# Three blocks on one core: weights as the stationary operand in FFN steps 2 to 9 and in the second heads' queries and keys

## The chip, the core and the metric

The kernel runs on one core of one Trainium2 chip. The metric is the device time of one execution in microseconds (us): three runs gave 985.66, 987.0 and 992.59 us, median 987.0 us. The profiled execution took 987.64 us, of which the span of its instructions is 985.9 us.

## The reference

For 256 tokens of width 1024 in float32, the reference runs three residual blocks one behind the other: a first block with a mixer of convolution and forgetting attention, and the two layers of block 2, one with blockwise attention (moba) and one with differential attention (diff). Each ends in a gated feed-forward network (FFN). What the change touches is this:

```python
def swiglu_2(h, w_in, w_out):
    g, u = jnp.split(h @ w_in, 2, axis=-1)
    return (jax.nn.silu(g) * u) @ w_out
...
    q, k, v = jnp.split(h @ w_qkv, 3, axis=-1)
```

The hidden width of every FFN is 2816. Block 2 modulates its norms by shift, scale and gate vectors, `c_act @ ada_w[i] + ada_b[i]`, which depend on the inputs alone and not on the tokens' way through the blocks.

## The kernel before, in words

**Products in three parts.** A float32 operand is split into a high part (rounded to the type fp32r by ScalarE) and a low part (what is left, subtracted by VectorE). A product is high by high, high by low and low by high, three matmuls into one bank of PSUM. The tokens' transposed activations are `hT` (high `hTh`, low `hTl`); each 128x512 piece of weights, a unit, gets its tiles `hi`/`lo` (or `wp`, a second pool that is open in the FFNs) as it arrives.

**The usual way round.** In `product` and `triple` the 128 tokens of one half are the stationary operand and 512 columns of weights move past them. The result has tokens on the partitions. Where the next product contracts over those columns, TensorE has to transpose the result, 128x128 at a time, by a matmul against `ident` (recorded under L151; all other matmuls stand under L145).

**The FFN.** It has 11 steps of 256 hidden columns. In `up(s, h)` the 8 units of step s (256 gate and 256 up columns side by side) are used for token half h: 24 matmuls of 512 columns into one bank. `activate` then takes Silu on ScalarE, multiplies on VectorE, has two transposes made, and splits the result into a tile `pair`. `downs(s)` multiplies by 4 units of the second matrix: 24 matmuls of 512 columns, which add into four banks held through the whole FFN. Steps 0 and 1 go first; from step 2 on the order is `up(s, 0)`, `up(s, 1)`, then `downs(s-1)` up to s = 8; `up(9)` stands without one; step 10 and the last three `downs` end the FFN, one token half after the other.

**Queries and keys in block 2.** Heads 0 to 3 are made the usual way. Those of heads 4 to 7 already go the other way round in `turned_product`: 128 columns of weights are stationary and the 256 tokens move, so the result has the columns on the partitions and needs no transposes. Two banks hold four heads' results, and `keep_turned` copies them out on ScalarE, 512 columns at a time.

**The order.** Every engine's order is fixed when the program is built. The class `Order` keeps a clock of its own, which the matmuls drive; after each matmul `pump` lets the waiting tasks (activations, softmax, `ada`) issue their next instruction, and then `fill` issues the splitting of the next weights. `Lane` holds one engine's order and its costs. On the chip each engine goes through its list in order and waits where its inputs aren't there. SyncE's queue loads all weights, 16 pairs of `hi`/`lo` tiles and in the FFNs 8 more pairs hold those that are split ahead of use. The `ada` task spreads the modulation vectors' 192 multiply-adds on VectorE (`asum<-araw`) over the program; each of their 24 halves ends in four transposes or two matmuls on TensorE. PSUM has 8 banks; in an FFN four of them are the held ones.

Of the kernel before, what the change touches and what calls it, by code (L numbers as in the profile page):

```python
# [13 lines left out]
F32R = mybir.dt.float32r  # L14
AF = mybir.ActivationFunctionType
OP = mybir.AluOpType
# [4 lines left out]
P = 128  # L21
# [197 lines left out]
def block_kernel(ctx: ExitStack, tc: tile.TileContext, a: dict, onehot: bass.AP, out: bass.AP):  # L219
# [12 lines left out]
    def small(name, shape, dtype=F32):  # L232
        return cst.tile(shape, dtype, name=name)
# [20 lines left out]
    hT = (small("hTh", [P, NKT, 256], F32R), small("hTl", [P, NKT, 256], F32R))  # L254
# [152 lines left out]
    def turned_product(us, blocks, marks):  # L407

        for k, u in enumerate(us):
            for h in range(2):
                o.wait(marks[h][k // 4])
            u.uses = 1
            wh, wl = use(u)
            xh, xl = hT[0][:, k], hT[1][:, k]
            last = k == len(us) - 1
            for ps, cs in blocks:
                for i, c in enumerate(cs):  # L420
                    out, w = ps[:, i * 256:(i + 1) * 256], slice(c, c + P)
                    o.mm(out, wh[:, w], xh, k == 0 and i == 0, False, True)
                    o.pump()
                    o.mm(out, wh[:, w], xl, False, False, True)
                    o.pump()
                    t = o.mm(out, wl[:, w], xh, False, last and i == len(cs) - 1, True)
                    o.pump()
            u.pool.give(u.slot, t)
        return t
# [662 lines left out]
    def ffn(hm, gb, **kw):  # L1092
        ys = []
        acts, act_mark, us_of, dn = {}, {}, {}, {}
# [3 lines left out]
        def activate(s, h, ps):  # L1098
# [16 lines left out]
            act_mark[s, h].t = split(acts[s][:, h], acts[s][:, 2 + h], tp[:, :256])  # L1115
            banks.give(tp, act_mark[s, h].t)

# [8 lines left out]
        def down(s, h, n):  # L1126
            if s not in dn:
                dn[s] = take(1)
            o.wait(act_mark[s, h])
            for j in range(2):  # L1130
                c = slice(j * P, (j + 1) * P)
                t = triple(ys[h][n][0], acts[s][:, h, c], acts[s][:, 2 + h, c], dn[s][2 * j + n],
                           s == 0 and j == 0, s == STEPS - 1 and j == 1)
            if s == STEPS - 1:
                ys[h][n][1].t = t
            if h and n:
                pairs.give(acts[s], t)
# [11 lines left out]
        for s in range(2, STEPS - 1):  # L1149
            up(s, 0)  # L1150
            up(s, 1)
            if s - 1 < STEPS - LAG:
                downs(s - 1)
# [47 lines left out]
    def attention(l, hm, gb, **kw):  # L1201
# [14 lines left out]
        qk_mark = {(n, i, h): Mark() for n in range(2) for i in range(2) for h in range(2)}  # L1216
# [21 lines left out]
        def keep_turned(n, i, bs):  # L1238
            while qks.when() is None or qks.when() > o.now:
                yield o.now + 0.1  # L1240
            qk[n, i] = qks.take()
            for j, b in enumerate(bs):
                r = A.activation(qk[n, i][:, 2 * j:2 * j + 2], b.rearrange("p (j t) -> p j t", t=256), AF.Copy,
                                 scale=1.0 if i else d ** -0.5)
                banks.give(b, r)
            for h in range(2):
                qk_mark[n, i, h].t = r
# [3 lines left out]
        def head(n, j):  # L1251
            hd = n * 4 + j
            yield from o.until(tb_mark[hd // 2], *(qk_mark[n, i, h] for i in range(2) for h in range(2)))
# [36 lines left out]
        for i in range(2):  # L1290
            bs = [o.hold(banks) for _ in range(2)]
            t = turned_product(take(2), [(b, (2 * j * P, (2 * j + 1) * P)) for j, b in enumerate(bs)], hm)
            o.spawn(keep_turned(1, i, bs), t)
# [105 lines left out]
```

## Time and profile before

| | |
|---|---|
| median of three runs | 987.0 us |
| profiled execution | 987.64 us |
| span of its instructions | 985.9 us |
| TensorE busy | 976.0 us, 99% |
| weight loads busy | 805.9 us, 82% |
| VectorE busy | 739.6 us, 75% |
| ScalarE busy | 605.1 us, 61% |
| DMA engines busy, weights' queue | 67.9% |

The ends of matmuls are modelled in this profile, so a recorded matmul is longer than its share of the engine: a matmul's price is the distance from its start to the next one's start. TensorE's granted clock was 0.999 of its full speed over the span.

### The profile page before, as it was taken

The numbers are of one execution on the slowest core, as the hardware profiler recorded it, in microseconds if no ns is written. First come the engines' busy times: TensorE is split into PE (matmuls) and PEld (weight loads), VectorE is DVE, ScalarE is ACT, GpSimd is POOL, SyncE is SP. The second block draws the span as 40 slices with busy tenths as digits, with TensorE's granted clock in tenths as the row PEclk, the third lists the DMA queues.
The fourth block names the chain that finished last, engine by engine and source line by source line (L and its number), as shares of the span: only waits on it lengthen the run. The fifth ranks groups of instructions, "written<-read, shape, count | busy, mean of one in ns | idle before, by whom it ended". The sixth has DMA issues, their size and how long they took to land.

```text
span 985.9 us, 14069 instructions
## 1 busy us (share of the span) xinstructions
PE 976.0 (99%) x4826; PEld 805.9 (82%) x4826; DVE 739.6 (75%) x1470; ACT 605.1 (61%) x1286; POOL 35.4 (4%) x65
## 2 busy tenths in 40 slices
PE   9999999999999999999999999999999999999997
PEld 6888778888888878898888888888897888888885
DVE  6789789989888868887899888637766796464632
ACT  7756675765546437866775554537878785454631
POOL 1000000000000001000000000001000100000000
PEclk9999999999999999999999999999999999999999
DMA  7977777679988874784779989636542657556401
GB/s 244 345 240 263 258 281 238 232 226 344 349 279 303 300 272 170 270 297 153 243 223 324 349 287 322 224 106 222 180 137 82 198 196 261 200 166 206 161 22 44
DMA packets 143637, 227.22 MB, mean 230 GB/s; under 512 B 6087, under 2 KB 79028, under 8 KB 143564
## 3 DMA queue, kind: packets, MB, share of 16 engines
q1 hardware_dynamic: 143548, 226.30, 67.9%
q8 instruction: 38, 0.62, 0.3%
q14 instruction: 35, 0.29, 0.1%
q10 hardware_dynamic: 16, 0.00, 0.0%
HBM read 225.22 MB, written 2.63 MB: 231 GB/s over the span
## 4 chain that ended last, share of the span: by engine, by line
PE 90%; DMA 3%; DVE 3%; issue 2%; ACT 1%; SPq 0%; POOL 0%; DVEq 0%; POOLq 0%; ACTq 0%
PE bank L145 85%; PE bank L151 5%; DMA araw<-in_ada_w_dram 2%; DVE asum L89 1%; DVE lo L89 1%; DMA x<-in_x_dram 1%; DVE wp L89 0%; ACT hi L89 0%; SPq L137 0%; DMA raw<-in_w_in_dram 0%; DVE x L89 0%; DVE ch L89 0%; ACT junk L89 0%; POOL tiny L89 0%; ACT L89 0%
## 5 line engine op out<-in xcount | busy, mean ns | idle before, releaser
L89 DVE TENSOR_TENSOR lo<-raw,hi 128x512 fp32r<-128x512 f32 (+1 forms) x499 | 322.9, 677 | 35.8 <-ACT hi L89 34.1
L89 ACT ACTIVATE hi<-raw 128x512 fp32r<-128x512 f32 (+1 forms) x499 | 298.0, 621 | 59.8 <-PE bank L145 35.2
L145 PE MATMUL bank<-hi,hTh 128*128 128x512 f32 (+1 forms) x670 | 262.7, 392 | 0.5 <-ACT hTh L89 0.5
L145 PE MATMUL bank<-hi,hTl 128*128 128x512 f32 (+1 forms) x670 | 261.8, 391 | 0.2 <-DVE hTl L89 0.2
L145 PE MATMUL bank<-lo,hTh 128*128 128x512 f32 (+1 forms) x670 | 261.0, 389 | 0.0
L145 PE MATMUL bank<-hi,pair 128*128 128x512 f32 x528 | 173.5, 394 | 0.0
L89 DVE SCALAR_TENSOR_TENSOR asum<-araw,c_act,asum 128x512 f32<-128x512 f32 x192 | 143.3, 746 | 7.9 <-DMA araw<-in_ada_w_dram 7.2
L145 PEld LDWEIGHTS bank<-hi,hTl 128*128 128x128 f32 x670 | 125.9, 188 | 26.1 <-issue 1.3
L145 PEld LDWEIGHTS bank<-lo,hTh 128*128 128x128 f32 x670 | 126.0, 188 | 24.2 <-DVE lo L89 0.8
L145 PEld LDWEIGHTS bank<-hi,hTh 128*128 128x128 f32 x670 | 125.9, 188 | 24.2 <-ACT hTh L89 1.3
L145 PE MATMUL bank<-wp,hTh 128*128 128x512 f32 x388 | 120.4, 391 | 0.0
L145 PEld LDWEIGHTS bank<-hi,pair 128*128 128x128 f32 x528 | 98.0, 188 | 19.7 <-issue 0.2
L89 ACT ACTIVATE ep<-bank 128x256 f32<-128x256 f32 x66 | 25.4, 384 | 131.8 <-PE bank L145 131.3
L145 PE MATMUL bank<-lo,pair 128*128 128x512 f32 x264 | 103.6, 393 | 0.0
L89 ACT ACTIVATE wp<-raw 128x512 fp32r<-128x512 f32 x145 | 88.9, 630 | 22.4 <-PE bank L145 16.4
L89 DVE TENSOR_TENSOR wp<-raw,wp 128x512 fp32r<-128x512 f32 x145 | 95.2, 686 | 8.8 <-ACT wp L89 8.6
L145 PEld LDWEIGHTS bank<-wp,hTh 128*128 128x128 f32 x388 | 72.5, 188 | 15.1
L89 DVE TENSOR_TENSOR ep<-ep,bank 128x256 f32<-128x256 f32 x70 | 29.2, 417 | 66.7 <-ACT ep L89 66.4
L145 PE MATMUL bank<-wp,hTl 128*128 128x512 f32 x194 | 75.9, 391 | 0.0
L145 PE MATMUL bank<-wp,pair 128*128 128x512 f32 x288 | 75.8, 396 | 0.0
L145 PEld LDWEIGHTS bank<-wp,pair 128*128 128x128 f32 x288 | 53.0, 188 | 10.4
L89 DVE TENSOR_TENSOR pair<-bank,pair 128x256 fp32r<-128x256 f32 (+1 forms) x74 | 32.5, 439 | 37.3 <-ACT pair L89 36.7
(131 smaller groups left out, 953.6 us busy)
## 6 DMA issues: line engine op xcount, KB each, us to landing
araw<-in_ada_w_dram SPq DMA_DIRECT2D x96, 512.0 KB
raw<-in_ffn_w_in_dram SPq DMA_DIRECT2D x88, 512.0 KB
raw<-in_w_gate_up_dram SPq DMA_DIRECT2D x44, 512.0 KB
raw<-in_ffn_w_out_dram SPq DMA_DIRECT2D x22, 1024.0 KB
raw<-in_w_in_dram SPq DMA_DIRECT2D x16, 1024.0 KB
raw<-in_moba_w_qkv_dram SPq DMA_DIRECT2D x12, 1024.0 KB
raw<-in_diff_w_qkv_dram SPq DMA_DIRECT2D x12, 1024.0 KB
raw<-in_w_down_dram SPq DMA_DIRECT2D x11, 1024.0 KB
```

The lines of the kernel that those rows point to most:

```text
L89: self.order.pin(self, fn(out, *args, **kw))
L145: self.pin(self.pe, self.nc.tensor.matmul(out, lhsT, rhs, start=start, stop=stop, skip_group_check=shared))
L151: self.pin(self.pe, self.nc.tensor.transpose(out, src, ident))
```

## The change

`hTh` and `hTl` become the two halves of one tile `hTb`, so that the high and the low part of the 256 tokens of one row of pieces lie side by side. `turned_product` then makes one matmul of 512 columns (the weights' high part against both parts of the tokens; the left half of the bank gets high by high, the right half high by low) and one of 256 columns (the weights' low part against the tokens' high part, into the left half). The two halves of the bank are added on the way out. One bank now holds 128 columns of the result.

This serves heads 4 to 7 (two passes over the weights, two heads each), and, new, FFN steps 2 to 9: `up_turned` makes, for each 128 of the step's 256 hidden columns, a bank of gate and a bank of up columns. `activate_turned` copies both left halves out on ScalarE, adds both right halves on VectorE, takes Silu, multiplies and splits. The result has the hidden columns on its partitions already, as `downs` wants it.

```diff
--- before.py
+++ after.py
@@ -251,7 +251,8 @@
 
     pairs = ring(cst, "pair", 4, [P, 4, 256], F32R)
     x = [small(f"x{h}", [P, D]) for h in range(2)]
-    hT = (small("hTh", [P, NKT, 256], F32R), small("hTl", [P, NKT, 256], F32R))
+    hT_both = small("hTb", [P, NKT, 2, 256], F32R)
+    hT = hT_both[:, :, 0], hT_both[:, :, 1]
 
 
     stream = []
@@ -412,20 +413,15 @@
         for k, u in enumerate(us):
             for h in range(2):
                 o.wait(marks[h][k // 4])
-            u.uses = 1
             wh, wl = use(u)
-            xh, xl = hT[0][:, k], hT[1][:, k]
-            last = k == len(us) - 1
-            for ps, cs in blocks:
-                for i, c in enumerate(cs):
-                    out, w = ps[:, i * 256:(i + 1) * 256], slice(c, c + P)
-                    o.mm(out, wh[:, w], xh, k == 0 and i == 0, False, True)
-                    o.pump()
-                    o.mm(out, wh[:, w], xl, False, False, True)
-                    o.pump()
-                    t = o.mm(out, wl[:, w], xh, False, last and i == len(cs) - 1, True)
-                    o.pump()
-            u.pool.give(u.slot, t)
+            for ps, c in blocks:
+                w, last = slice(c, c + P), k == len(us) - 1
+                o.mm(ps, wh[:, w], hT_both[:, k].rearrange("p i t -> p (i t)"), k == 0, False, True)
+                o.pump()
+                t = o.mm(ps[:, :256], wl[:, w], hT[0][:, k], False, last, True)
+                o.pump()
+            if not u.uses:
+                u.pool.give(u.slot, t)
         return t
 
     allk = range(NKT)
@@ -1091,7 +1087,7 @@
 
     def ffn(hm, gb, **kw):
         ys = []
-        acts, act_mark, us_of, dn = {}, {}, {}, {}
+        acts, act_mark, turned_mark, us_of, dn = {}, {}, {}, {}, {}
         last = kw.pop("last", False)
         out_marks = None if last else marks2()
 
@@ -1112,8 +1108,40 @@
                     acts[s] = pairs.take()
                 else:
                     yield o.now + 0.1
-            act_mark[s, h].t = split(acts[s][:, h], acts[s][:, 2 + h], tp[:, :256])
+            c = slice(h * P, (h + 1) * P)
+            act_mark[s, h].t = split(acts[s][:, 0:2, c], acts[s][:, 2:4, c], tp[:, :256].rearrange("p (j t) -> p j t", t=P))
             banks.give(tp, act_mark[s, h].t)
+
+        def activate_turned(s, j, bg, bu):
+
+            e = yield from o.get(st)
+            g, u = e[:, :256], e[:, 256:512]
+            r = A.activation(g, bg[:, :256], AF.Copy)
+            r2 = A.activation(u, bu[:, :256], AF.Copy)
+            yield r
+            r = V.tensor_add(g, g, bg[:, 256:])
+            banks.give(bg, r)
+            yield max(r, r2)
+            r2 = V.tensor_add(u, u, bu[:, 256:])
+            banks.give(bu, r2)
+            yield max(r2, A.activation(g, g, AF.Silu))
+            r = V.tensor_mul(g, g, u)
+            yield r
+            while s not in acts:
+                if pairs.when() is not None and pairs.when() <= o.now:
+                    acts[s] = pairs.take()
+                else:
+                    yield o.now + 0.1
+            turned_mark[s, j].t = split(acts[s][:, j], acts[s][:, 2 + j], g)
+            st.give(e, turned_mark[s, j].t)
+
+        def up_turned(s):
+            us = take(2)
+            for j in range(2):
+                turned_mark[s, j] = Mark()
+                bs = [(o.hold(banks), c) for c in (j * P, 256 + j * P)]
+                t = turned_product(us, bs, hm)
+                o.spawn(activate_turned(s, j, bs[0][0], bs[1][0]), t)
 
         def up(s, h):
             if s not in us_of:
@@ -1126,10 +1154,10 @@
         def down(s, h, n):
             if s not in dn:
                 dn[s] = take(1)
-            o.wait(act_mark[s, h])
+            c = slice(h * P, (h + 1) * P)
             for j in range(2):
-                c = slice(j * P, (j + 1) * P)
-                t = triple(ys[h][n][0], acts[s][:, h, c], acts[s][:, 2 + h, c], dn[s][2 * j + n],
+                o.wait(turned_mark[s, j] if (s, j) in turned_mark else act_mark[s, h])
+                t = triple(ys[h][n][0], acts[s][:, j, c], acts[s][:, 2 + j, c], dn[s][2 * j + n],
                            s == 0 and j == 0, s == STEPS - 1 and j == 1)
             if s == STEPS - 1:
                 ys[h][n][1].t = t
@@ -1147,8 +1175,7 @@
         ys += [[(o.hold(banks), Mark()) for _ in range(2)] for _ in range(2)]
         downs(0)
         for s in range(2, STEPS - 1):
-            up(s, 0)
-            up(s, 1)
+            up_turned(s)
             if s - 1 < STEPS - LAG:
                 downs(s - 1)
         us_of[STEPS - 1] = take(2)
@@ -1213,7 +1240,7 @@
 
         o.spawn(position_bias())
         qk, pts = {}, [ptp.take() for _ in range(2)]
-        qk_mark = {(n, i, h): Mark() for n in range(2) for i in range(2) for h in range(2)}
+        qk_mark = {(n, i, h): Mark() for n in range(2) for i in range(2) for h in range(4 if n else 2)}
         pt_mark = [[Mark() for _ in range(4)] for _ in range(2)]
 
         def keep_qk(n, i, h, ps):
@@ -1235,22 +1262,24 @@
             m.t = A.activation(qk[n, i][:, :, h * P:(h + 1) * P], tp.rearrange("p (j t) -> p j t", t=P), AF.Copy)
             banks.give(tp, m.t)
 
-        def keep_turned(n, i, bs):
-            while qks.when() is None or qks.when() > o.now:
-                yield o.now + 0.1
-            qk[n, i] = qks.take()
-            for j, b in enumerate(bs):
-                r = A.activation(qk[n, i][:, 2 * j:2 * j + 2], b.rearrange("p (j t) -> p j t", t=256), AF.Copy,
-                                 scale=1.0 if i else d ** -0.5)
-                banks.give(b, r)
-            for h in range(2):
-                qk_mark[n, i, h].t = r
+        def keep_turned(n, i, j, b):
+            while (n, i) not in qk:
+                if qks.when() is not None and qks.when() <= o.now:
+                    qk[n, i] = qks.take()
+                else:
+                    yield o.now + 0.1
+            scale = 1.0 if i else d ** -0.5
+            t = qk[n, i][:, j]
+            yield A.activation(t, b[:, :256], AF.Copy, scale=scale)
+            r = V.scalar_tensor_tensor(t, b[:, 256:], scale, t, op0=OP.mult, op1=OP.add)
+            banks.give(b, r)
+            qk_mark[n, i, j].t = r
 
         scored = {}
 
         def head(n, j):
             hd = n * 4 + j
-            yield from o.until(tb_mark[hd // 2], *(qk_mark[n, i, h] for i in range(2) for h in range(2)))
+            yield from o.until(tb_mark[hd // 2], *(qk_mark[n, i, h] for i in range(2) for h in ([j] if n else range(2))))
             q, k, bias = qk[n, 0][:, j], qk[n, 1][:, j], tb[hd // 2][:, (hd % 2) * 256:(hd % 2) * 256 + 256]
             sums = tiny_tile()[:, :4].rearrange("p (c i) -> p c i", c=2)
             rows_of = [slice(c * 64, c * 64 + d) for c in range(l + 1)]
@@ -1288,9 +1317,12 @@
                 group(us[i], 512, lambda h, ps, i=i: keep_qk(0, i, h, ps), hm, (h,))
         o.spawn(heads(0), o.now + 2.0)
         for i in range(2):
-            bs = [o.hold(banks) for _ in range(2)]
-            t = turned_product(take(2), [(b, (2 * j * P, (2 * j + 1) * P)) for j, b in enumerate(bs)], hm)
-            o.spawn(keep_turned(1, i, bs), t)
+            us = take(2)
+            for j0 in (0, 2):
+                bs = [(o.hold(banks), j * P) for j in (j0, j0 + 1)]
+                t = turned_product(us, bs, hm)
+                for ps, c in bs:
+                    o.spawn(keep_turned(1, i, c // P, ps), t)
         o.spawn(heads(1), o.now + 2.0)
 
         vs, v_mark = {}, {(h, n): Mark() for h in range(2) for n in range(2)}
```

Three places show how the instructions now stand.

TensorE in the last FFN, inside a step, where the second token half begins (`bank3` is the first half's product, `bank1` the second's, `ep1` the first half's activation). Before:

```order
L145 MATMUL bank3_66<-hi5_86,hTl_171 128x512
L145 MATMUL bank1_64<-hi1_78,hTh_170 128x512
L145 MATMUL bank1_64<-lo1_79,hTh_170 128x512
L145 MATMUL bank1_64<-hi1_78,hTl_171 128x512
L145 MATMUL bank1_64<-hi0_76,hTh_170 128x512
L145 MATMUL bank1_64<-lo0_77,hTh_170 128x512
L145 MATMUL bank1_64<-hi0_76,hTl_171 128x512
L151 MATMUL bank5_68<-ident_197,ep1_116 128x128 x2
L145 MATMUL bank1_64<-hi2_80,hTh_170 128x512
```

With the change, in the same FFN, from the last product of `downs` into the next step (`bank2` gate, `bank1` up columns):

```order
L145 MATMUL bank7_70<-lo4_85,pair2_166 128x512
L145 MATMUL bank7_70<-hi4_84,pair2_166 128x512
L145 MATMUL bank2_65<-hTb_170,hi2_80 128x512
L145 MATMUL bank2_65<-hTb_170,lo2_81 128x256
L145 MATMUL bank1_64<-hTb_170,hi2_80 128x512
L145 MATMUL bank1_64<-hTb_170,lo2_81 128x256
L145 MATMUL bank2_65<-hTb_170,hi8_92 128x512
L145 MATMUL bank2_65<-hTb_170,lo8_93 128x256
```

The transposes of `ep` are gone from steps 2 to 9 (96 in the program), and each unit now stands as four matmuls for 128 hidden columns, two of 512 and two of 256 columns, in place of three of 512 for 128 tokens.

VectorE in the first FFN, during a step (`lo` and `wp` are weights being split, `asum` is `ada`, `ep` and `pair` are the activation). Before:

```order
L89 TENSOR_TENSOR lo7_91<-raw2_73,hi7_90 128x512
L89 TENSOR_TENSOR lo10_97<-raw2_73,hi10_96 128x512
L89 SCALAR_TENSOR_TENSOR asum1_122<-araw1_75,c_act_211,asum1_122 128x512
L89 TENSOR_TENSOR ep2_117<-ep2_117,bank2_65 128x256
L89 TENSOR_TENSOR lo11_99<-raw0_71,hi11_98 128x512
L89 SCALAR_TENSOR_TENSOR asum1_122<-araw1_75,c_act_211,asum1_122 128x512
L89 TENSOR_TENSOR pair1_165<-bank1_64,pair1_165 128x256
L89 TENSOR_TENSOR lo12_101<-raw0_71,hi12_100 128x512
```

With the change (`st2` is the activation of one half, `bank7` and `bank1` its gate and up columns):

```order
L89 SCALAR_TENSOR_TENSOR asum0_121<-araw1_75,c_act_210,asum0_121 128x512
L89 TENSOR_TENSOR wp1_1647<-raw1_72,wp0_1646 128x512
L89 SCALAR_TENSOR_TENSOR asum0_121<-araw1_75,c_act_210,asum0_121 128x512
L89 TENSOR_TENSOR st2_110<-st2_110,bank7_70 128x256
L89 TENSOR_TENSOR lo12_101<-raw2_73,hi12_100 128x512
L89 TENSOR_TENSOR st2_110<-st2_110,bank1_64 128x256
L89 TENSOR_TENSOR lo13_103<-raw2_73,hi13_102 128x512
L89 TENSOR_TENSOR lo14_105<-raw2_73,hi14_104 128x512
L89 TENSOR_TENSOR st2_110<-st2_110 128x256
L89 TENSOR_TENSOR lo0_77<-raw2_73,hi0_76 128x512
L89 SCALAR_TENSOR_TENSOR asum0_121<-araw0_74,c_act_210,asum0_121 128x512
L89 TENSOR_TENSOR pair0_164<-st2_110,pair0_164 128x256
```

Where one half of a step had two instructions (product and split), it now has four: two additions out of PSUM, the product and the split. In the whole program this is 96 more, and 16 more for the queries and keys.

TensorE in layer 1 of block 2, in the queries of heads 4 to 7. Before:

```order
L145 MATMUL bank4_67<-lo10_97,hTh_170 128x512
L145 MATMUL bank4_67<-hi10_96,hTl_171 128x512
L145 MATMUL bank2_65<-hTh_170,hi11_98 128x256
L145 MATMUL bank2_65<-hTl_171,hi11_98 128x256
L145 MATMUL bank2_65<-hTh_170,lo11_99 128x256
```

With the change (`bank7` and `bank2` are two heads):

```order
L145 MATMUL bank2_65<-hTb_170,hi7_90 128x512
L145 MATMUL bank2_65<-hTb_170,lo7_91 128x256
L145 MATMUL bank7_70<-hTb_170,hi8_92 128x512
L145 MATMUL bank7_70<-hTb_170,lo8_93 128x256
L145 MATMUL bank2_65<-hTb_170,hi8_92 128x512
L145 MATMUL bank2_65<-hTb_170,lo8_93 128x256
L145 MATMUL bank7_70<-hTb_170,hi9_94 128x512
```

For one head and one unit, three matmuls of 256 columns have become one of 512 and one of 256.

## Rows read from the trace of the kernel before

**Rows 1.** The page: engines' busy time, and the chain that ended last by engine.

```profile
PE 976.0 (99%) x4826; PEld 805.9 (82%) x4826; DVE 739.6 (75%) x1470; ACT 605.1 (61%) x1286; POOL 35.4 (4%) x65
...
PE 90%; DMA 3%; DVE 3%; issue 2%; ACT 1%; SPq 0%; POOL 0%; DVEq 0%; POOLq 0%; ACTq 0%
```

**Rows 2.** Busy time by stretch: the FFNs' steps, then second heads' queries and keys.

```profile
core 0: us, PE busy (x) PEld busy (x) DVE busy (x) ACT busy (x) POOL busy (x), PEclk, DMA share, GB/s
212.00:346.00 134.00, 133.75 (x613) 109.75 (x612) 118.35 (x202) 71.54 (x133) 3.69 (x7) 1.00 0.93 315
513.00:648.00 135.00, 134.77 (x614) 110.69 (x613) 110.05 (x188) 69.89 (x129) 2.63 (x5) 1.00 0.87 298
819.00:954.00 135.00, 135.00 (x610) 110.97 (x609) 73.64 (x128) 68.93 (x125) 0.00 (x0) 1.00 0.52 172
408.00:431.00 23.00, 23.00 (x186) 22.63 (x185) 21.82 (x52) 18.43 (x44) 0.53 (x1) 1.00 0.82 286
```

**Rows 3.** Waits over the span: us in total, times, longest us.

```profile
PE bank L151 <- DVE ep L89: 0.5, 2, 0.3
PE bank L151 <- DVE asum L89: 0.5, 1, 0.5
...
PEld bank L145 <- DVE lo L89: 1.5, 5, 0.4
```

**Rows 4.** Chain of waits, last FFN: start us, us, what. One step, then the sixth after.

```profile
835.57 10.48 PE bank L145 x46
846.05 0.22 PE bank L151 x2
846.27 5.95 PE bank L145 x26
852.22 0.22 PE bank L151 x2
852.44 10.47 PE bank L145 x46
...
936.72 10.48 PE bank L145 x46
```

**Rows 5.** Timeline of TensorE in that step: start us, us, what.

```profile
839.09 0.39 PE L145 MATMUL bank<-hi,hTh 128*128 128x512 f32 x1
...
845.66 0.39 PE L145 MATMUL bank<-hi,hTl 128*128 128x512 f32 x1
845.89 0.38 PE L151 MATMUL bank<-ident,ep 128*128 128x128 f32 x2
846.03 0.48 PE L145 MATMUL bank<-hi,hTh 128*128 128x512 f32 x1
846.34 0.40 PE L145 MATMUL bank<-lo,hTh 128*128 128x512 f32 x1
```

**Rows 6.** Timeline of TensorE, second heads of layer 1: a switch of widths, then 256 alone.

```profile
421.83 0.28 PE L145 MATMUL bank<-hTh,hi 128*128 128x256 f32 x1
421.95 0.40 PE L145 MATMUL bank<-hi,ones_r 128*128 128x512 f32 x1
422.18 0.39 PE L145 MATMUL bank<-lo,ones_r 128*128 128x512 f32 x1
422.41 0.28 PE L145 MATMUL bank<-hTl,hi 128*128 128x256 f32 x1
422.53 0.28 PE L145 MATMUL bank<-hTh,lo 128*128 128x256 f32 x1
...
427.00 0.28 PE L145 MATMUL bank<-hTl,hi 128*128 128x256 f32 x1
...
430.96 0.28 PE L145 MATMUL bank<-hTl,hi 128*128 128x256 f32 x1
```

**Rows 7.** The page's groups: the weight loads, line, engine, count, busy us, mean ns.

```profile
L145 PEld LDWEIGHTS bank<-hi,hTl 128*128 128x128 f32 x670 | 125.9, 188 | 26.1 <-issue 1.3
```

**Rows 8.** Timeline of VectorE in the first FFN: start us, us, what.

```profile
335.52 3.10 DVE L89 TENSOR_TENSOR wp<-raw,wp 128x512 fp32r<-128x512 f32 x5
338.53 0.41 DVE L89 TENSOR_TENSOR ep<-ep,bank 128x256 f32<-128x256 f32 x1
338.86 0.75 DVE L89 SCALAR_TENSOR_TENSOR asum<-araw,c_act,asum 128x512 f32<-128x512 f32 x1
```

**Rows 9.** Timeline of ScalarE there.

```profile
336.75 0.38 ACT L89 ACTIVATE ep<-bank 128x256 f32<-128x256 f32 x1
337.03 0.62 ACT L89 ACTIVATE hi<-raw 128x512 fp32r<-128x512 f32 x1
```

**Rows 10.** Timeline of TensorE in the first FFN: transposes for `ada`.

```profile
347.48 0.39 PE L145 MATMUL bank<-hi,hTh 128*128 128x512 f32 x1
348.32 0.66 PE L151 MATMUL bank<-ident,asum 128*128 128x128 f32 x4 [0.45 <-DVE asum L89]
```

## The prediction, on record before the changed kernel had run

> **What bounds the kernel now.** I read the page first: TensorE is busy for 99% of the span and makes 90% of the chain that ended last, while VectorE and ScalarE stand at 75% and 61% [rows 1]. Then the stretches: in all three FFNs TensorE has no free time, VectorE is at 88% in the first (118.35 of 134 us), 82% in the second and 55% in the third [rows 2]. Then the waits: weight loads waited for split weights for 1.5 us in the whole program, and TensorE for an activation or for `ada` sums for 0.5 us each [rows 3]. So neither weights nor activations are late, and the time is the sum of what stands in TensorE's own list. In the last FFN the chain shows nothing else: 46 matmuls, 2 transposes, 26 matmuls, 2 transposes, and again; from 835.57 to 936.72 us six such steps take 16.86 us each [rows 4]. That makes the forecast a count of matmuls times the distance between their starts.
>
> **Prices, from starts.** From 839.09 to 845.66 us stand 30 matmuls of 512 columns: 6.57 / 29 = 0.2266 us each [rows 5]. From 427.00 to 430.96 us stand 34 matmuls of 256 columns: 3.96 / 33 = 0.1200 us [rows 6]. Two transposes with two matmuls of 512 take 846.34 - 845.66 = 0.68 us; less 2 x 0.2266, a transpose costs 0.113 us [rows 5]. A step by these prices is 72 x 0.2266 + 4 x 0.113 = 16.77 us; the measured 16.86 us leaves 0.09 us, which I put down to the breaks that the transposes make, since matmuls run at the bare price elsewhere.
>
> The TensorE page of the Trainium skill ("TensorE: Matmul & The Clock Gate", section on the back-to-back issue gap) gives N / 2.4 + 2.5 ns, so 216 and 109 ns. The rows show 11 ns more for either width, so a matmul more costs more here than the page has it. By the page's figures the sum below would be -12.4 us, an estimate; the rows decide.
>
> **FFN steps 2 to 9: 8 steps in 3 FFNs, 24 in all.** *Matmuls.* 48 of 512 columns become 32 of 512 and 32 of 256: the same columns, 16 instructions more. 32 x 0.2266 + 32 x 0.1200 - 48 x 0.2266 = +0.21 us a step. *Transposes.* Four fewer: -0.45 us, and -0.09 us with the breaks. A step becomes 16.53 us, 0.33 us less; 24 x 0.33 = **-7.9 us**. All of it is on the path, because TensorE is.
>
> That price of a short matmul is from a stretch of short ones alone; in the new order they alternate with long ones. A switch from 256 to 512 and back, at 421.83 to 422.53 us, takes 0.70 us for two of each, against 0.693 by the prices [rows 6]: up to 3.5 ns for a switch, which may be rounding. 896 pairs with two switches each bound that at +6.3 us. Below, a short matmul could go as fast as a transpose, 0.113 us: 896 x 0.007 = -6.3 us. I take nothing, since the row of the switch lies nearest to nothing. If the breaks' 0.09 us stays, the gain is 2.2 us smaller.
>
> **Queries and keys of heads 4 to 7, two layers.** 192 matmuls of 256 columns (23.04 us) become 64 of 512 and 64 of 256 (22.18 us): -0.86 us a layer, **-1.7 us**. The weights are now gone through twice, so 8 units are wanted in half the time. They are split while heads 0 to 3 run, and the loads hardly wait for splits today [rows 3], so I cost that at nothing. If this cover fails, the first pass waits for VectorE at 0.60 us a unit against 0.69 us of use, which it still keeps up with.
>
> **VectorE.** In each half of a step, two instructions become four: an addition of 256 columns out of PSUM takes 338.86 - 338.53 = 0.33 us of VectorE's list, a split of 512 columns 3.01 / 5 = 0.60 us [rows 8]. Taking 0.34 us for all of them, a step gains 1.36 us and an FFN 10.9 us. In the first FFN that makes some 129 busy of 131 us, in the second 121 of 132, in the third 85 of 132 [rows 2]. ScalarE gains two copies at 0.28 us in a half [rows 9], 9 us an FFN, and stays near 80 of 131. I cost this at nothing on the path: what VectorE does here is split weights that stand ready ahead of use and `ada` sums that are wanted much later, and both can move back. The new chain (copy, add, Silu, multiply, split) has six links, but `downs(s)` stands behind `up(s+1)` and `downs(s-1)`, 16.5 us later, and a half's two banks come back into use only after the other half and a `downs`, some 11 us later. In the second heads of layer 1, 8 more instructions meet a VectorE that is busy for 21.82 of 23 us [rows 2]; there `ada` moves back, and the matmuls for the values cover the heads' softmax. DMA moves the same bytes, in the same order on SP's queue; POOL's queue is as before.
>
> **Sum.** -7.9 - 1.7 = -9.6 us against the profiled execution's own 987.64 us: **978.0 us**. The median shown, 987.0 us, is 0.6 us below that execution, so against it this is -0.9%. About 1% is what a measurement here can tell from no change; that bound lies at 977.1 us, close to my number.
>
> **Rivals.**
> *A part is given back in the first two FFNs (0.20).* With 129 of 131 us busy, VectorE falls behind its list whenever a link of the new chain makes it wait, and TensorE, whose order is fixed, waits where an `ada` sum's transposes stand, as it did at 347.48 us for 0.45 us with less load [rows 10]. Half or all of seven such places in each of two FFNs at that price are 3 to 6 us: 981 to 984 us. Against it: today's total of such waits is 0.5 us [rows 3].
> *VectorE becomes the bound: slower (0.07).* If waits between the engines eat the 15.65 us that VectorE has free in the first FFN, and likewise in the second, then its added 10.9 us shows in full twice: 987.6 - 9.6 + 21.8 = 1000 us. The point is where split weights are no longer ready ahead; the 1.5 us of waiting for them speaks against it, the 88% for it.
> *Short matmuls are cheaper between long ones (0.10).* At 0.113 us: 972 us.
> *The weight loads show (0.03).* There are 160 more of them in the program (1792 for the new matmuls against 1632 for the matmuls and transposes removed), and each is recorded at 188 ns [rows 7], longer than a short matmul's 120. If one must end before its matmul starts, 896 pairs lose 0.068 us each: +61 us, 1039 us. Against it: the short stretch ran at 0.120 us with a load for every matmul [rows 6]. The same page of the skill (section on LDWEIGHTS) has the load at its columns / 1.2, an estimate of 107 ns here, which would just fit under a short matmul; that agrees with the rows' pace and not with the recorded 188 ns.
> That the change doesn't do what it says is excluded by the order, where the 96 transposes are gone.
>
> **How the numbers follow.** The forecast (0.60) has its own range, 975 to 981 us, from a small part of the two bounds on the alternation and the breaks' 2.2 us. The predicted time is its 978.0. The range goes up over the first rival to 984.5 us and down to 973 us, most of the way to the third. Faster by over 1%: a little under half of the forecast, 0.29, and the cheap short matmuls, 0.10, together 0.39. Within 1%: the rest of the forecast, 0.31, and the first rival, 0.20, together 0.51. Slower by over 1%: 0.07 + 0.03 = 0.10.
>
> **What would show it.** Right: in the last FFN the chain has a period of 16.5 us and no L151 from steps 2 to 9; a pair of 512 and 256 columns takes 0.347 us from start to start; TensorE still at 99%; VectorE above 95% in the first FFN with weight loads' waits for `lo` still a few us. Wrong: a pair that takes clearly more or less than 0.347 us; gaps on TensorE before `ada`'s transposes; weight loads that wait for splits or for banks given late by the new additions.

## The result, and the profile after

The changed kernel takes 981.98 us (median of 11 runs, 981.5 to 983.57), the kernel before 987.96 us beside it (11 runs, 985.66 to 992.59): a ratio of 0.9942 [0.9929, 0.9955], or -6.0 us by the medians. The time lies in the range forecast and the direction is right, but 9.6 us had been worked out. The profiled execution took 983.57 us with a span of 981.8 us; it is the slowest of the eleven. It began with a wait of 1.2 us for the first tokens, which the waits below show.

The page of the changed kernel, engines and chain [rows 1], and its groups for the new matmuls (the group's columns: busy us, mean ns, idle us before it):

```profile
PE 970.9 (99%) x4986; PEld 810.4 (83%) x4986; DVE 773.7 (79%) x1582; ACT 622.3 (63%) x1390; POOL 34.7 (4%) x65
...
PE 93%; issue 2%; DMA 2%; ACT 1%; DVE 1%; SPq 0%; POOL 0%; DVEq 0%; POOLq 0%; ACTq 0%
...
L145 PE MATMUL bank<-hTb,hi 128*128 128x512 f32 x612 | 219.7, 398 | 0.0
...
L145 PE MATMUL bank<-hTb,lo 128*128 128x256 f32 x612 | 172.9, 283 | 0.0
```

TensorE is still the bound, with a larger share of the chain. VectorE has 34.1 us more in 112 instructions more, 0.30 us each.

The same three stretches of the FFNs [rows 2] (us of the stretch, busy us of PE, PEld, DVE, ACT and POOL, the granted clock, the DMA engines' busy share, GB/s):

```profile
212.00:346.00 134.00, 134.00 (x707) 114.39 (x706) 124.49 (x228) 74.46 (x159) 3.68 (x7) 1.00 0.92 309
513.00:648.00 135.00, 135.00 (x719) 115.50 (x717) 124.39 (x227) 75.34 (x160) 3.15 (x6) 1.00 0.89 304
819.00:954.00 135.00, 135.00 (x709) 115.01 (x708) 81.69 (x156) 75.32 (x155) 0.00 (x0) 1.00 0.50 165
```

TensorE has no free time in any of them, at full granted clock. VectorE went from 118.35, 110.05 and 73.64 us to these. The first FFN gained less than the second: `ada`'s multiply-adds went from 58 to 60 in the first stretch and from 50 to 58 in the second, while the weights split in the first fell from 102 to 97.

The waits [rows 3], TensorE's own and that of the weight loads for splits:

```profile
PE bank L151 <- DMA x<-in_x_dram: 1.2, 1, 1.2
PE bank L145 <- DVE logf L89: 1.1, 1, 1.1
...
PEld bank L145 <- DVE lo L89: 1.1, 3, 0.4
...
PE bank L145 <- ACT hTb L89: 0.9, 1, 0.9
...
PE bank L151 <- DVE ch L89: 0.4, 1, 0.4
```

The waits of before for `ep` and `asum`, 0.5 us in total for each, are gone, and none for a bank or an addition took their place.

The chain of waits in the last FFN [rows 4] (start us, us, what), and TensorE's timeline of one step there [rows 5] (start us, recorded us, instruction):

```profile
815.21 139.62 PE bank L145 x727
954.82 0.22 PE bank L151 x2
```

```profile
835.74 0.39 PE L145 MATMUL bank<-hTb,hi 128*128 128x512 f32 x1
835.97 0.28 PE L145 MATMUL bank<-hTb,lo 128*128 128x256 f32 x1
836.08 0.40 PE L145 MATMUL bank<-hTb,hi 128*128 128x512 f32 x1
...
836.79 0.40 PE L145 MATMUL bank<-hTb,hi 128*128 128x512 f32 x1
...
837.14 0.40 PE L145 MATMUL bank<-hTb,hi 128*128 128x512 f32 x1
...
837.49 0.40 PE L145 MATMUL bank<-hTb,hi 128*128 128x512 f32 x1
...
837.85 0.40 PE L145 MATMUL bank<-hTb,hi 128*128 128x512 f32 x1
...
847.03 0.40 PE L145 MATMUL bank<-hi,pair 128*128 128x512 f32 x1
...
852.54 0.39 PE L145 MATMUL bank<-hTb,hi 128*128 128x512 f32 x1
```

No transpose stands in 139.62 us, as forecast. But the step's 32 pairs take 847.03 - 835.74 = 11.29 us, 0.353 us a pair and not 0.347, and the step's period is 852.54 - 835.74 = 16.80 us, not 16.53. The pairs are not alike: from 836.79 us on they take 0.35, 0.35 and 0.36 us, and this repeats through the step, so every third pair is the long one. The same 64 matmuls in the same order in the second FFN:

```profile
536.95 0.40 PE L145 MATMUL bank<-hTb,hi 128*128 128x512 f32 x1
537.18 0.28 PE L145 MATMUL bank<-hTb,lo 128*128 128x256 f32 x1
...
548.04 0.40 PE L145 MATMUL bank<-hi,pair 128*128 128x512 f32 x1
```

Here they take 11.09 us, 0.3466 us a pair, which is the forecast's price, and no pair takes 0.36 us. So one order of matmuls has two rhythms. Of the 24 steps, less the `ada` matmuls and transposes that stand in some, 19 take 11.26 to 11.29 us, four take 11.09 to 11.12, and one is mixed at 11.19. All eight of the last FFN are slow, where VectorE is busy for 60%; three of the fast ones stand in the second, where it is busy for 92%. A busier VectorE is then not what makes a step slow. Nor is it the pool that the weights lie in: pairs from `hi`/`lo` and from `wp` stand in steps of both rhythms. Their sum is 270.05 us where 24 x 11.09 = 266.2 was forecast: +3.9 us.

### The profile page after: what moved, and what is told of

The parts are those of the page before. It is cut to its first block, busy times and chain, and to the rows that moved or that the text cites. A ratio compares the mean times of both kernels' runs of the same rounds, so it can differ in the third digit from the quotient of the medians.

```text
span 981.8 us, 14543 instructions
## 1 busy us (share of the span) xinstructions
PE 970.9 (99%) x4986; PEld 810.4 (83%) x4986; DVE 773.7 (79%) x1582; ACT 622.3 (63%) x1390; POOL 34.7 (4%) x65
## 4 chain that ended last, share of the span: by engine, by line
PE 93%; issue 2%; DMA 2%; ACT 1%; DVE 1%; SPq 0%; POOL 0%; DVEq 0%; POOLq 0%; ACTq 0%
PE bank L145 89%; PE bank L151 4%; ACT hi L89 1%; DMA bf<-in_b_f_dram 1%; DMA x<-in_x_dram 1%; DVE lo L89 0%; SPq L137 0%; ACT junk L89 0%; DMA raw<-in_w_in_dram 0%; DVE x L89 0%; DVE ch L89 0%; POOL tiny L89 0%; ACT L89 0%; ACT hTb L89 0%; DVE hTb L89 0%
## 5 line engine op out<-in xcount | busy, mean ns | idle before, releaser
L145 PE MATMUL bank<-hi,hTb 128*128 128x512 f32 (+1 forms) x820 | 259.5, 389 | 0.9 <-ACT hTb L89 0.9
L145 PE MATMUL bank<-hTb,hi 128*128 128x512 f32 x612 | 219.7, 398 | 0.0
L145 PEld LDWEIGHTS bank<-hi,hTb 128*128 128x128 f32 x820 | 150.4, 188 | 30.2 <-issue 1.5
L145 PE MATMUL bank<-hTb,lo 128*128 128x256 f32 x612 | 172.9, 283 | 0.0
L145 PE MATMUL bank<-lo,hTb 128*128 128x512 f32 (+1 forms) x410 | 159.3, 389 | 0.0
L145 PEld LDWEIGHTS bank<-hTb,hi 128*128 128x128 f32 x612 | 114.9, 188 | 27.0 <-issue 0.3
L145 PEld LDWEIGHTS bank<-hTb,lo 128*128 128x128 f32 x612 | 115.6, 189 | 1.7 <-issue 0.7
L145 PE MATMUL bank<-hTb,wp 128*128 128x512 f32 (+1 forms) x568 | 108.6, 339 | 0.0
L145 PEld LDWEIGHTS bank<-hTb,wp 128*128 128x128 f32 x568 | 87.3, 188 | 13.1
L145 PEld LDWEIGHTS bank<-lo,hTb 128*128 128x128 f32 x410 | 77.1, 188 | 14.0 <-issue 0.5
```

Source lines behind the costliest of these rows:

```text
L145: self.pin(self.pe, self.nc.tensor.matmul(out, lhsT, rhs, start=start, stop=stop, skip_group_check=shared))
```

## The experiments

Every diff is against the changed kernel; ratios are against the kernel before, which took 988 us beside them.

### The two parts alone

`e1_ffn_only` leaves the queries and keys of heads 4 to 7 as before (three matmuls of 256 columns); `e2_heads_only` leaves the FFNs as before.

```diff
 e1_ffn_only
-            us = take(2)
-            for j0 in (0, 2):
...
-                t = turned_product(us, bs, hm)
+            bs = [o.hold(banks) for _ in range(2)]
+            t = turned_short(take(2), [(b, (2 * j * P, (2 * j + 1) * P)) for j, b in enumerate(bs)], hm)
 e2_heads_only
-            up_turned(s)
+            up(s, 0)
+            up(s, 1)
```

> The FFN steps as changed; the queries and keys of heads 4 to 7 made as before, with three matmuls of 256 columns and no halves to add. Theory 1 (TensorE's list alone sets the time, and a pair of a long and a short matmul takes 0.353 us where 0.347 was forecast): the FFNs give 24 steps x (0.54 for transposes and breaks - 0.40 for the matmuls) = -3.5 to -4.9 us, so 983 to 984.5 us where the kernel before has 988.0 and the changed one 982.0. Rival (the added work on VectorE costs time in the first two FFNs, and the heads bring the gain): under 2 us of gain, 986 us or more.

> The queries and keys of heads 4 to 7 as changed; all FFN steps as before, with their transposes. Theory 1: the matmuls of the two turned stretches took 24.11 and 24.07 us before and 23.61 and 23.44 us with the change, so -1.1 us: 986.9 us. Rival of the first experiment: -4 us, 984 us.

Measured: the FFNs alone 983.42 us, 0.995 [0.9937, 0.9963]; the heads alone 985.92 us, 0.9979 [0.997, 0.9987]. So the FFNs bring some 4.8 us (3.7 to 6.2 by the interval) and the heads some 2 us (1.3 to 3.0). Both parts gain, and the shortfall lies in the FFNs, whose forecast was 7.9. In the traces of before and after, the heads' 128 matmuls went from 24.11 and 24.07 us to 23.61 and 23.44: -1.1 us together, where -1.7 was forecast.

The trace of `e1_ffn_only` shows one thing more. From step 2 of the first FFN on, its list on TensorE is the changed kernel's for 760 matmuls (144 us), and each of them starts within 0.001 us of the changed kernel's, counted from the first. The rhythm of each step is therefore no chance of one execution; it comes again with the list.

### Is it the alternation? Long and short matmuls in groups

The same matmuls and bytes, in another order within `turned_product`. In `e3_long_then_short` all 16 long ones of a pair of banks come first, then their 16 short ones; `e4_two_units` and `e5_one_unit` group by two units (4 long, 4 short) and by one (2 and 2), by the number in the condition (the cut shows `e3_long_then_short`). `e6_same_bank` has 2 long and 2 short into one bank, then the same into the other.

```diff
...
+            held.append((k, u, wh, wl))
             for ps, c in blocks:
-                w, last = slice(c, c + P), k == len(us) - 1
-                o.mm(ps, wh[:, w], hT_both[:, k].rearrange("p i t -> p (i t)"), k == 0, False, True)
+                o.mm(ps, wh[:, c:c + P], hT_both[:, k].rearrange("p i t -> p (i t)"), k == 0, False, True)
                 o.pump()
-                t = o.mm(ps[:, :256], wl[:, w], hT[0][:, k], False, last, True)
-                o.pump()
...
+            if len(held) == 8:
+                for k2, u2, _, wl2 in held:
+                    for ps, c in blocks:
+                        t = o.mm(ps[:, :256], wl2[:, c:c + P], hT[0][:, k2], False, k2 == len(us) - 1, True)
+                        o.pump()
...
+                held = []
```

> The changed kernel with one difference: for each pair of banks the 16 matmuls of 512 columns of all 8 units stand first, then the 16 of 256 columns, so widths switch twice per pair of banks in place of 32 times. The work is the same. Theory 1a (the 6 ns by which a pair is dearer than its two prices come from switching widths): 24 x 2 + 8 blocks of 16 pairs win 0.006 us a pair, 896 x 0.006 = -5.4 us against the changed kernel: 976.5 us. Rival 1b (TensorE falls into a slower rhythm for another reason, such as other engines' traffic): no change, 982 us. Rival 1c (weights are freed later, in a burst, and the next ones come late): slower, 983 to 986 us.

> As the run before, but two units at a time: four matmuls of 512 columns, then four of 256, so 8 switches per pair of banks in place of 32. Theory 1a: three quarters of the 5.4 us, 978 us. Rival 1b: 982 us. Rival 1c: 982 us, since weights are freed almost as early as in the changed kernel.

> As e3, but one unit at a time: long into the first bank, long into the second, short into the first, short into the second. 32 switches of width in a step where the changed kernel has 64, and never the same bank twice running. In the last FFN a step's 64 new matmuls took 11.29 us in the changed kernel, 11.20 in e4 (16 switches) and 11.10 in e3 (4). Theory 1a' (switches make the slower rhythm): between the changed kernel and e4, 11.20 to 11.29 us. Rival 1d (what is dear is two matmuls of unlike width into the same bank, one behind the other): 11.20 us or less, as e4, since no bank comes twice running.

> Two units at a time, but bank after bank: two long and two short into the first bank, then into the second. 32 switches in a step, as e5, and the same bank four times running. Theory 1a': the same as e5. Rival 1d: as the changed kernel or slower, 11.29 us.

| | switches of width in a step | a step's 64 matmuls, last FFN | time, median | ratio |
|---|---|---|---|---|
| changed kernel | 64 | 11.29 us | 981.98 | 0.9942 [0.9929, 0.9955] |
| `e4_two_units` | 16 | 11.20 | 981.34 | 0.993 [0.9918, 0.9942] |
| `e5_one_unit` | 32 | 11.14 | 980.25 | 0.992 [0.9905, 0.9936] |
| `e6_same_bank` | 32 | 11.14 | 979.41 | 0.9911 [0.9896, 0.9926] |
| `e3_long_then_short` | 4 | 11.11 | 979.77 | 0.9918 [0.9904, 0.9931] |

TensorE in the last FFN of `e3_long_then_short`, the step's start, the first short ones, `downs`, and the next step:

```profile
833.40 1.07 PE L145 MATMUL bank<-hTb,hi 128*128 128x512 f32 x4
...
837.03 0.64 PE L145 MATMUL bank<-hTb,lo 128*128 128x256 f32 x4
...
844.51 0.40 PE L145 MATMUL bank<-hi,pair 128*128 128x512 f32 x1
...
849.98 0.39 PE L145 MATMUL bank<-hTb,hi 128*128 128x512 f32 x1
```

The 64 matmuls take 844.51 - 833.40 = 11.11 us, the forecast's 11.09 within 0.02, and the period is 16.58 us against 16.53. So the prices taken from before hold within 0.02 us when 16 of one width stand together. The time fell less: 976.5 us was expected from 6 ns on each of 896 pairs, and 979.77 came. In the trace the matmuls of the 24 steps are some 3 us shorter together, and TensorE waits 0.4 us for `fm` and 1.1 us for `ch`, where the changed kernel has no wait for `fm` and 0.4 us for `ch`. In `e6_same_bank` the rhythm is this:

```profile
833.08 0.62 PE L145 MATMUL bank<-hTb,hi 128*128 128x512 f32 x2
833.53 0.40 PE L145 MATMUL bank<-hTb,lo 128*128 128x256 f32 x2
833.76 0.63 PE L145 MATMUL bank<-hTb,hi 128*128 128x512 f32 x2
...
844.22 0.40 PE L145 MATMUL bank<-hi,pair 128*128 128x512 f32 x1
```

And a step of `e4_two_units`, then one of `e5_one_unit`, from the first matmul to the first of `downs`:

```profile
834.10 1.07 PE L145 MATMUL bank<-hTb,hi 128*128 128x512 f32 x4
...
845.30 0.40 PE L145 MATMUL bank<-hi,pair 128*128 128x512 f32 x1
```

```profile
834.20 0.62 PE L145 MATMUL bank<-hTb,hi 128*128 128x512 f32 x2
...
845.34 0.40 PE L145 MATMUL bank<-hi,pair 128*128 128x512 f32 x1
```

The runs of `e6_same_bank`, 979.38 to 979.69 us, all lie below every run of the changed kernel, by 2.6 us in the median; `e3_long_then_short` lies within 0.4 us of it. A fixed cost for each switch of width is ruled out: 16 switches (`e4_two_units`, 11.20 us) cost more than 32 (`e5_one_unit`, 11.14 us). So is the bank: 2 and 2 take 11.14 us whether the bank changes inside the group or not. The times don't follow the steps alone: `e5_one_unit` has the steps of `e6_same_bank` and is 0.8 us slower by the medians, and in its trace TensorE waits 0.6 us before transposes of `ada`, the kind of wait that the prediction's first rival feared.

### Does a rhythm last? One break in a step

The second of the 8 units has its 2 long matmuls first and then its 2 short ones, the others alternate as in the changed kernel.

```diff
+            for ps, w in ws:
+                long(ps, w)
+                if k != 1:
+                    t = short(ps, w)
+            if k == 1:
+                for ps, w in ws:
+                    t = short(ps, w)
```

> The changed kernel, but the second of each eight units stands in the order long, long, short, short; the other seven keep long, short, long, short. In the trace of the changed kernel two steps ran at 0.347 us a pair throughout, and two went over from 0.353 to 0.347 us where two other matmuls of 512 columns stood between. Theory S (TensorE keeps the rhythm it is in until something breaks it): all units behind the second run at 0.347, a step's 64 matmuls take 11.11 us, 978 us. Rival P (each pattern has its own pace): one unit of eight gains, 11.27 us, 981.5 us.

Measured: 981.86 us, 0.9937 [0.9919, 0.9954], the steps of the last FFN 11.19 us, all eight alike. That is between the two expectations, 11.11 and 11.27. TensorE in one of them: the break in the first half with the alternation behind it up to the second half's break, and the alternation behind that:

```profile
835.76 0.64 PE L145 MATMUL bank<-hTb,hi 128*128 128x512 f32 x2
...
837.16 0.40 PE L145 MATMUL bank<-hTb,hi 128*128 128x512 f32 x1
...
841.32 0.62 PE L145 MATMUL bank<-hTb,hi 128*128 128x512 f32 x2
...
842.73 0.40 PE L145 MATMUL bank<-hTb,hi 128*128 128x512 f32 x1
...
846.26 0.40 PE L145 MATMUL bank<-hi,pair 128*128 128x512 f32 x1
```

From 837.16 to 841.32 us stand 12 pairs at 0.347 us, from 842.73 to 846.26 us 10 pairs at 0.353. So a rhythm, once there, lasts through many pairs, and a break can set it. But the second break, with the same matmuls, left the slow rhythm behind it. In the changed kernel's first FFN it likewise went from slow to fast behind two matmuls that `ada` put in, at 277.77 us; two such in the next step did not bring the fast one. What decides which rhythm follows a break is open.

### The transposes' price

`e3_long_then_short` with the four transposes put back into every step; their results are not read. It stands against `e3_long_then_short`, so that the rhythm doesn't mix in.

```diff
             yield r
+            tp = yield from o.get(banks)
+            for i in range(2):
+                r = o.tr(tp[:, i * P:(i + 1) * P], g[:, i * P:(i + 1) * P], ident)
+            banks.give(tp, r)
+            yield r
             while s not in acts:
```

> e3 with four transposes put back into each of the 24 steps: each half's product is turned into a bank that nobody reads, and the split waits for it; the activation itself is split as in e3. Theory 1 (TensorE's list is the time; a transpose is 0.113 us and its break 0.02): 24 x 0.54 = +13 us against e3's 979.8: 992.8 us; without the breaks' part +10.8, 990.6 us. Rival (transposes went into gaps, so taking them away gave little): 980 to 985 us.

Measured: 991.96 us, 1.0038 [1.0023, 1.0053], 12.2 us over `e3_long_then_short`; 12.2 / 24 = 0.51 us a step. Its chain in the last FFN:

```profile
833.65 8.08 PE bank L145 x43
841.73 0.22 PE bank L151 x2
841.95 8.57 PE bank L145 x45
850.52 0.22 PE bank L151 x2
850.74 8.08 PE bank L145 x43
```

The period is 850.74 - 833.65 = 17.09 us against 16.58, so again 0.51 us for four. The forecast had 0.54, 0.45 for the transposes and 0.09 for their breaks. The term holds within 0.03 us a step, breaks and all.

### Does VectorE's added work cost anything?

`e11_no_adds` leaves out the additions of the halves, so the product of high weights and low tokens is missing from the FFN's steps 2 to 9. `e8_vector_double` makes each addition a second time, into the bank, where nobody reads it.

```diff
 e11_no_adds
-            r = V.tensor_add(g, g, bg[:, 256:])
             banks.give(bg, r)
-            yield max(r, r2)
-            r2 = V.tensor_add(u, u, bu[:, 256:])
             banks.give(bu, r2)
 e8_vector_double
-            r = V.tensor_add(g, g, bg[:, 256:])
+            V.tensor_add(g, g, bg[:, 256:])
+            r = V.tensor_add(bg[:, 256:], g, bg[:, 256:])
             banks.give(bg, r)
             yield max(r, r2)
-            r2 = V.tensor_add(u, u, bu[:, 256:])
+            V.tensor_add(u, u, bu[:, 256:])
+            r2 = V.tensor_add(bu[:, 256:], u, bu[:, 256:])
```

> The changed kernel without the additions of the halves in the FFN steps, so that high by low is left out of their sums; 96 instructions fewer on VectorE, and TensorE's matmuls unchanged. The double additions cost 4.8 us. Theory 1 (the changed kernel is just below the point from which VectorE's work counts): 981 to 982 us. Rival 2 (VectorE's work counts already, in proportion): 977 us.

> The changed kernel with the two additions of each half made twice, the second time into the bank's right half, where nobody reads them: 96 instructions more on VectorE, as many as the FFN part of the change added there net. Theory 1 (VectorE's work costs nothing on the path while weights are split ahead of use): 982 us, under 1 us more. Rival 2 (VectorE is at its end in the first two FFNs, and part of the forecast gain was lost there): the first two FFNs lose as much again, +4 us or more, 986 us.

Measured without them: 983.59 us, 0.996 [0.9943, 0.9976], no faster than the changed kernel, and by the medians 1.6 us slower, with intervals that overlap. The 977 us of the rival did not come. VectorE's busy time in the first FFN fell, in the windows of `e11_no_adds`, and TensorE stayed full:

```profile
212.00:346.00 134.00, 134.00 (x707) 114.11 (x706) 117.21 (x201) 78.22 (x161) 3.69 (x7) 1.00 0.92 314
```

So the forecast's nothing for VectorE is right. With them twice: 986.8 us, 0.9984 [0.9974, 0.9993], 4.8 us over the changed kernel, as the rival there expected (986). In the trace of `e8_vector_double` most of it is one place in the second FFN, where VectorE is busy for 128.75 of 135 us. First TensorE's timeline there (the bracket: idle us, and what ended it), then VectorE's, then the windows (busy us of PE, PEld, DVE, ACT and POOL, then the granted clock):

```profile
577.96 0.77 PE L145 MATMUL bank<-hTb,hi 128*128 128x512 f32 x1 [2.28 <-DVE bank L89]
578.52 0.41 PE L145 MATMUL bank<-hTb,lo 128*128 128x256 f32 x1
578.74 0.63 PE L145 MATMUL bank<-hTb,hi 128*128 128x512 f32 x1
```

```profile
576.28 0.74 DVE L89 SCALAR_TENSOR_TENSOR asum<-araw,c_act,asum 128x512 f32<-128x512 f32 x1
576.94 0.41 DVE L89 TENSOR_TENSOR st<-st,bank 128x256 f32<-128x256 f32 x1
577.38 0.43 DVE L89 TENSOR_TENSOR bank<-st,bank 128x256 f32<-128x256 f32 x1
```

```profile
575.00:580.00 5.00, 2.72 (x10) 2.10 (x10) 4.21 (x10) 1.46 (x4) 0.53 (x1) 0.76 1.02 322
580.00:590.00 10.00, 10.00 (x50) 8.47 (x49) 9.11 (x18) 4.29 (x10) 0.00 (x0) 0.95 0.89 294
```

VectorE is late in its list: the additions that free a bank stand behind `ada` work, and TensorE waits 2.28 us for that bank. At the end of the wait the granted clock is down, to a mean of 0.76 over the 5 us around it and 0.95 over the next 10, and the long matmul takes 0.56 us to the next start, the short one 0.22, together 0.78 us where a pair has 0.35: the lower level (1.2 GHz). The step there takes 15.57 us, where another with four transposes of `ada` takes 11.73: 3.8 of the 4.8 us. So VectorE's margin ends within 32 more additions an FFN, and that shows as a bank given late, not as weights split late. That VectorE as a whole would then be the bound is not shown: it is one place in one trace, and the first FFN lost nothing like it.

### What do the halves side by side bring?

The FFN the other way round but with three matmuls of 256 columns, gate and up in one bank, nothing to add, and the activation straight out of PSUM.

```diff
+                    o.mm(out, wh[:, w], xh, k == 0 and i == 0, False, True)
+                    o.pump()
+                    o.mm(out, wh[:, w], xl, False, False, True)
+                    o.pump()
+                    t = o.mm(out, wl[:, w], xh, False, last and i == len(cs) - 1, True)
...
-        def activate_turned(s, j, bg, bu):
+        def activate_turned(s, j, ps):
+            e = yield from o.get(ep)
+            t = e[:, :256]
+            yield A.activation(t, ps[:, :256], AF.Silu)
+            r = V.tensor_mul(t, t, ps[:, 256:])
```

> FFN steps 2 to 9 with the weights stationary, but as the second heads were made before the change: three matmuls of 256 columns into one sum, gate and up columns side by side in one bank, no halves to add, so two additions and two copies fewer in each half. Heads as changed. A step has 96 matmuls of 0.120 us, 11.52 us, against 11.25 measured in the mean. Theory 1 (TensorE's list is the time): 24 x 0.27 = +6.5 us, 988.5 us. Rival 2 (the halves' additions on VectorE cost as much as they save): 982 us or less.

Measured: 989.14 us, 1.0006 [0.9992, 1.0019], 7.2 us over the changed kernel. In its trace's last FFN, the first matmul of a step and of its `downs`:

```profile
839.99 0.40 PE L145 MATMUL bank<-hTb,hi 128*128 128x256 f32 x2
...
851.50 0.40 PE L145 MATMUL bank<-hi,pair 128*128 128x512 f32 x1
```

96 matmuls take 11.51 us, 0.120 each as before [rows 6]. That is 0.22 us a step over the slow rhythm and 0.42 over the fast one. The heads keep their gain in this run, and still the time is that of before. So turning the FFN's products round without widening them would have gained nothing: by the prices 96 x 0.120 us is 0.64 us more than 48 x 0.2266 us, and the transposes with their breaks give 0.51 to 0.54.

## Why the prediction was right, and where its size was off

**What bounds the kernel: right.** TensorE's list is the time before and after. What was put on its list came through, 12.2 us for 96 transposes and 7.2 us for the short matmuls (6.5 expected), and taking VectorE's additions away brought nothing (`e11_no_adds`).

**The range: held in part by luck.** 981.98 us lies outside the forecast's own 975 to 981 and in the part up to 984.5 that the first rival added. That rival's waits before transposes of `ada` did not occur; a price came out higher instead.

**Matmuls: mis-sized.** The step that failed is the one on alternation: "I take nothing, since the row of the switch lies nearest to nothing." That row, 0.70 us for two of each, was a mix of the two widths, and read as it stood it gave 0.350 us a pair; I put the 3.5 ns a switch down to rounding. The measured pairs take 0.3528 us in the slow rhythm, 3.1 ns a switch, and 5 ns a pair on average: +3.9 us in the FFNs and some +0.6 in the heads. The upper bound of 6.3 us was the nearer end, but by luck: it isn't a price of a switch, since groups of 2 and 2 have half the switches of the changed kernel and lose only a quarter of what it loses (11.14 against 11.29, with 11.09 as the base). Every third pair is dearer, for a reason that no run here shows.

**Transposes: right**, 0.51 us a step against 0.54 (`e7_transposes_back`). The order with all long ones first has a `downs` of 849.98 - 844.51 = 5.47 us where 24 x 0.2266 = 5.44 was forecast; in the changed kernel it is 852.54 - 847.03 = 5.51, so up to 0.07 us a step of what had been put down to breaks stays there, at most 1.7 us in all. With this a step of the last FFN closes: 0.33 us forecast, less 0.20 for the pairs and 0.07 for `downs`, leaves 0.06, and its period went from 16.86 to 16.80 us.

**Rows against the Trainium skill.** The Trainium skill's rule for the back-to-back issue gap ("TensorE: Matmul & The Clock Gate") would make a pair an estimated 325 ns, and the whole sum -12.4 us; the trace does not agree, with 347 and 353 ns. The sum by rows was the nearer, and still too large.

**A gain that the sum left out.** The waits for `ep` and `asum`, 0.9 us together, are gone, 0.7 of it in the first FFN and 0.2 in the second. From step 2's first matmul to the first of the `downs` behind the first half of step 10, the FFNs took 139.21, 137.13 and 134.84 us before and 137.00, 135.92 and 134.35 with the change: gains of 2.2, 1.2 and 0.5 us, these waits included. With the heads' 1.1 that is 5.0 us; where the remaining 1.0 of the 6.0 by the medians lies is open.

**The rivals.** Waits for `ada` did not appear. VectorE as the bound did not decide here, but a late bank cost 3.8 us in one place with 96 additions more. Short matmuls were not cheaper between long ones. Weight loads didn't cost the 0.068 us a pair that this rival priced: pairs take 0.347 and 0.353 us, though each load is recorded at 188 ns. Whether the loads have a hand in the slow rhythm's 6 ns no run tests.

**Signs named ahead.** The chain without L151 and TensorE at 99% came as written; the waits for `lo` were 1.1 us, less than the few us named. The period (16.80, not 16.5) and the pair (0.353) were the signs of a mis-sized price. VectorE in the first FFN stands at 93%, not above 95%: 124.49 of 134 us.

## What to carry to other kernels

Where TensorE is full, price a new mix of matmul widths from a stretch with that mix, and if there is none, carry the few ns that a single switch leaves open as a part of the sum; then try the same matmuls in groups of two or more of one width, which here gave back 0.6 to 2.6 us for the same work. A transpose taken off a full TensorE pays what its place in the list costs, here 0.13 us with its break, as long as the engine that takes over its work has free time, and that margin can be measured by doubling the added work. A wait that hits a full TensorE can cost more than its length, as 2.28 us did here, because the clock comes back later: the step lost 3.8 us.

## What the runs showed of the hardware

The two rhythms were not expected: 64 matmuls, alternating between 512 and 256 columns, take 11.09 or 11.29 us in the same order, and a rhythm lasts over a whole step or several. In the slow one every third pair takes 0.36 us and the others 0.35. The same list brought the same rhythms in two kernels, to 0.001 us over 144 us. 4 and 4 take 11.20, 2 and 2 take 11.14, 16 and 16 take 11.11, and 96 of 256 columns 11.51 us. Neither the number of switches, nor the bank, nor the weights' pool, nor VectorE's load explains it; what sets it stays open. The second is the clock behind a wait: after 2.28 us without work on TensorE the granted clock's mean was 0.76 over the 5 us around its end and 0.95 over the next 10. The wait of 1.1 us for `logf` in the changed kernel left it at 1.00.
